# Attention with the two heads of a pair side by side: scores in 64-row tiles, one exponential for both, value matmuls adjacent in column halves

## Chip, cores and metric

The kernel runs on one NeuronCore of a Trainium2 chip. The metric is device time in microseconds (us) of one execution; the median of three runs of the kernel before is 2613.1 us (2609.99 to 2618.43). The profile shows one execution. Engines: PE is TensorE's matmul, PEld its weight load, DVE is VectorE, ACT is ScalarE, POOL is GpSimd, SP is SyncE, which here only issues DMAs.

## The reference, cut to what matters

The program is one layer with two branches: a recurrence (RWKV-7) and an attention with latent projections (MLA), mixed by gates. Sequence 2048, model width 1024. Only the attention is touched. It has 8 heads; each head's query and key have 64 plain features and 32 rotary ones, and the rotary part of the key is the same for all heads; a value has 64 features.

```python
def attend(args):
    qn, qp, b = args
    s = jnp.einsum('bqhd,bkhd->bhqk', qn, k_nope) + jnp.einsum('bqhr,bkr->bhqk', qp, k_pe)
    s = s.astype(jnp.float32) * scale
    q_idx = b * Q_BLOCK + jnp.arange(Q_BLOCK)
    s = jnp.where(key_idx[None, :] <= q_idx[:, None], s, jnp.finfo(jnp.float32).min)
    p = jax.nn.softmax(s, axis=-1).astype(dt)
    return jnp.einsum('bqhk,...' )  # weighted values, per head
```

## The kernel before

Phase 1 (0 to 1160 us) normalises the tokens, projects them and runs the recurrence. Phase 2 is the attention, phase 3 (from 1925 us) the gates and output projections. Everything in float32; where a matmul runs in the faster fp32r form, an operand is split into a leading part (names ending in H or h) and a trailing one (L or l), and a product is the sum of three (hi*hi, lo*hi, hi*lo).

The attention works on 4 pairs of heads, and for each pair on NS = 4 groups g of 512 queries. `queries(i)` (L933 to L980) prepares group i: projections `pq` (mm3, L277 to L279), the leading and trailing parts QH[h], QL[h] of each head (64 plain rows at the top, 32 rotary rows below, one row more for minus the row maximum), then the row maxima: for each head, each 128 queries j and each 512 keys c up to the diagonal a product `pm` of the leading parts (L966), on the diagonal with the causal mask added by a matmul (L969), and a maximum over the keys on DVE (L970). The maxima go through m, mh and `pn` (L978) into row 96 of QH (L979). `keys` (L905 to L917) makes a pair's keys. `attend(i)` (L1018 to L1084) goes through the keys in blocks kb of 128, 4g + 4 of them, and on the diagonal with only the queries that see them. For each head it computes scores transposed, keys on partitions, in three products into `pst` (L1040 to L1042; row 96 subtracts the row maximum), the mask (L1044), the exponential on ACT (L1050); one block later the value matmul into `po` (L1055), in float32, head 0 in the upper and head 1 in the lower column half of the array, and the running sum `acc` of the weights (L1060), on DVE for kb % 5 in (1, 3) and on POOL else. At the end of a group come the sums (L1068, psum_s) and `Ou`; at the end of a pair reciprocals and scaling (L1073 to L1083).

PSUM has 8 banks of 512 float32 per partition: here one for psum_s, one for po, two for pst and four for the tag "mx", which pm, pq, pk, pn and bc2 share. The loop (L1086 to L1106) writes the queries of up to two groups ahead before a group's attend. The order on each engine is set by a scheduler that goes by modelled times and by the pools' buffers; engines take their instructions in that order, and PE never passes one that waits.

## Time and profile before

| | |
|---|---|
| median of 3 runs | 2613.1 us |
| profiled execution: span | 2609.1 us |
| median of the runs less that span | 4.0 us, taken as what lies around the span; so the profiled execution's own time is 2613.1 us |
| busy: PE / DVE / ACT / POOL | 93% / 56% / 36% / 46% |
| attention: from, to, length | 1160, 1925, 765 us |

The busy shares are over the whole span. The granted clock (PEclk) is 1.00 at 2.4 GHz and 0.50 at 1.2 GHz. In the timeline a row is one instruction, or several in a row of the same group (x2); a matmul in float32 leaves two records. Matmuls overlap their ends, so the distance between two starts tells what one costs.

### The profile page before, as it was taken

The numbers are of one execution on the slowest core, as the hardware profiler recorded it, in microseconds if no ns is written. First come the engines' busy times: TensorE is split into PE (matmuls) and PEld (weight loads), VectorE is DVE, ScalarE is ACT, GpSimd is POOL, SyncE is SP. The second block draws the span as 40 slices with busy tenths as digits, with TensorE's granted clock in tenths as the row PEclk, the third lists the DMA queues.
The fourth block names the chain that finished last, engine by engine and source line by source line (L and its number), as shares of the span: only waits on it lengthen the run. The fifth ranks groups of instructions, "written<-read, shape, count | busy, mean of one in ns | idle before, by whom it ended". The sixth has DMA issues, their size and how long they took to land.

```text
span 2609.1 us, 36894 instructions
## 1 busy us (share of the span) xinstructions
PE 2430.6 (93%) x13097; PEld 1714.8 (66%) x13097; DVE 1453.1 (56%) x2527; ACT 945.0 (36%) x1806; POOL 1194.2 (46%) x1426
## 2 busy tenths in 40 slices
PE   7979999899979899998999999989989998999997
PEld 5757677677757667775445545545458886788886
DVE  7166785967677666636555555636343255632443
ACT  4344343433333333242243343323333332333331
POOL 6475665656564646435343343334223323333552
PEclk9989999899989999997999999999999999999999
DMA  6565464535444555443011011021044366543652
GB/s 214 155 208 138 128 202 118 140 84 152 111 125 104 146 135 149 113 130 95 19 38 35 23 37 53 19 99 49 0 140 130 94 210 193 176 135 97 200 179 77
DMA packets 395057, 303.42 MB, mean 116 GB/s; under 512 B 109372, under 2 KB 340856, under 8 KB 388984
## 3 DMA queue, kind: packets, MB, share of 16 engines
q1 hardware_dynamic: 364600, 252.30, 34.0%
q0 software_dynamic: 12992, 44.57, 5.3%
q10 hardware_dynamic: 17280, 4.20, 1.0%
q8 instruction: 103, 1.69, 0.3%
q14 instruction: 82, 0.67, 0.1%
HBM read 227.58 MB, written 73.40 MB: 115 GB/s over the span
## 4 chain that ended last, share of the span: by engine, by line
PE 66%; DVE 16%; DMA 9%; POOL 4%; issue 3%; ACT 2%; SPq 1%; ACTq 0%; POOLq 0%; DVEq 0%
PE po L1055 10%; PE pj L279 7%; PE pj L277 7%; PE pj L278 7%; PE pst L1040 4%; PE pm L966 3%; DVE tq L662 3%; DVE Xg L664 3%; DMA wraw<-in_w_in_dram 3%; PE pz L609 3%; PE pst L1042 3%; PE pst L1041 3%; PE pout L277 2%; PE py L277 2%; PE py L278 2%
## 5 line engine op out<-in xcount | busy, mean ns | idle before, releaser
L277 PE MATMUL pj<-xh,wh 128*128 128x512 f32 (+2 forms) x1344 | 539.3, 401 | 26.3 <-ACT wh L255 9.6
L279 PE MATMUL pj<-xh,wl 128*128 128x512 f32 (+2 forms) x1344 | 541.6, 403 | 3.6 <-POOL wl L256 3.5
L278 PE MATMUL pj<-xl,wh 128*128 128x512 f32 (+2 forms) x1344 | 536.4, 399 | 0.0
L256 POOL TENSOR_TENSOR wl<-wraw,wh 128x512 fp32r<-128x512 f32 (+1 forms) x266 | 345.4, 1300 | 353.3 <-ACT wh L255 325.9
L255 ACT CAST wh<-wraw 128x512 fp32r<-128x512 f32 x392 | 240.7, 614 | 530.3 <-PE pj L278 177.9
L277 PEld LDWEIGHTS pj<-xh,wh 128*128 128x128 f32 (+1 forms) x1344 | 259.5, 193 | 91.7 <-ACT wh L255 16.1
L1060 POOL TENSOR_TENSOR acc<-acc,pt 128x512 f32<-128x512 f32 (+3 forms) x160 | 175.6, 1100 | 292.4 <-ACT pt L1050 276.3
L279 PEld LDWEIGHTS pj<-xh,wl 128*128 128x128 f32 (+1 forms) x1344 | 259.4, 193 | 68.5 <-POOL wl L256 9.0
L278 PEld LDWEIGHTS pj<-xl,wh 128*128 128x128 f32 (+1 forms) x1344 | 259.4, 193 | 55.7 <-issue 1.6
L1050 ACT ACTIVATE pt<-pst 128x512 f32<-128x512 f32 (+3 forms) x288 | 150.9, 525 | 341.9 <-PE pst L1042 189.5
L970 DVE TENSOR_REDUCE mx<-pm 128x1 f32<-128x512 f32 (+2 forms) x320 | 180.3, 605 | 149.6 <-PE pm L966 99.9
L1055 PE MATMUL po<-pt,Vt 128*64 128x512 f32 (+3 forms) x576 | 260.8, 548 | 0.0
L256 DVE TENSOR_TENSOR wl<-wraw,wh 128x512 fp32r<-128x512 f32 x126 | 106.5, 848 | 100.3 <-ACT wh L255 99.9
L1060 DVE TENSOR_TENSOR acc<-acc,pt 128x512 f32<-128x512 f32 (+3 forms) x128 | 91.7, 722 | 112.7 <-ACT pt L1050 103.4
L1040 PEld LDWEIGHTS pst<-QH,KH 97*128 97x128 f32 x312 | 59.0, 189 | 135.4 <-ACT pt L1050 112.1
L1040 PE MATMUL pst<-QH,KH 97*128 97x512 f32 (+2 forms) x312 | 133.4, 428 | 12.4 <-ACT pt L1050 12.4
L1163 DVE SCALAR_TENSOR_TENSOR tg<-tg,py 128x512 f32<-128x512 f32 x64 | 43.8, 685 | 160.9 <-PE py L279 116.2
L662 DVE TENSOR_TENSOR tq<-Xg,Qg 128x30 f32<-128x30 f32 (+7 forms) x240 | 103.4, 431 | 32.6 <-DMA Xg<-d_q 26.6
L1042 PE MATMUL pst<-QH,KL 96*128 96x512 f32 (+2 forms) x312 | 115.1, 369 | 0.0
L1041 PE MATMUL pst<-QL,KH 96*128 96x512 f32 (+2 forms) x312 | 114.8, 368 | 0.0
L277 PE MATMUL py<-BH,wh 128*128 128x512 f32 x256 | 102.9, 402 | 8.2 <-DVE tg L1163 7.8
L966 PE MATMUL pm<-KH,QH 96*128 96x512 f32 (+2 forms) x312 | 108.8, 421 | 0.0
(356 smaller groups left out, 4479.4 us busy)
## 6 DMA issues: line engine op xcount, KB each, us to landing
wraw<-in_w_in_dram SPq DMA_DIRECT2D x320, 256.0 KB
cqt<-d_cq POOLq DMA_DIRECT2D x16, 1024.0 KB, 5.2
wfr<-in_w_o_dram SPq DMA_DIRECT2D x64, 256.0 KB
d_zg<-thg SPq DMA_DIRECT2D x42, 256.0 KB
xl<-d_x POOLq DMA_DIRECT2D x8, 1024.0 KB, 9.4
xh<-d_x POOLq DMA_DIRECT2D x8, 1024.0 KB, 9.5
ring<-in_x_dram SPq DMA_DIRECT2D x32, 256.0 KB
wraw<-in_w_out_a_dram SPq DMA_DIRECT2D x32, 256.0 KB
```

Source lines behind the costliest of these rows:

```text
L255: (ehi.copy if ehi is A else ehi.tensor_copy)(hi, src)
L256: elo.tensor_tensor(lo, src, f32(hi), op=ALU.subtract)
L277: PE.matmul(ps, lhsT=lh, rhs=rh, start=(i == 0), stop=False)
L278: PE.matmul(ps, lhsT=lh, rhs=rl, start=False, stop=False)
L279: PE.matmul(ps, lhsT=ll, rhs=rh, start=False, stop=(stop and i == n - 1))
L662: V.tensor_tensor(t3, Xg[:, 0:m, s_:s_ + 1].to_broadcast([P, m, n]), Qg[:, s_:s_ + 1, s_ + 1:32].to_broadcast([P, m, n]), op=ALU.mult)
L966: PE.matmul(pm[:, 0:w], lhsT=q_h[0:96, j * P:(j + 1) * P], rhs=kh[0:96, c * 512:c * 512 + w], start=True, stop=c < g)
L1040: PE.matmul(ps[:, q0:512], lhsT=kh[0:97, ks_], rhs=q_h[0:97, q0:512], start=True, stop=False)
L1041: PE.matmul(ps[:, q0:512], lhsT=kh[0:96, ks_], rhs=q_l[0:96, q0:512], start=False, stop=False)
L1042: PE.matmul(ps[:, q0:512], lhsT=kl[0:96, ks_], rhs=q_h[0:96, q0:512], start=False, stop=not diag)
L1055: PE.matmul(po[h * HD:(h + 1) * HD, q0:512], lhsT=Vt[p // 3][:, kb, (2 * p % 6 + h) * HD:(2 * p % 6 + h + 1) * HD], rhs=pts[h][:, q0:512], ...
L1060: e.tensor_tensor(acc[h][:, q0:512], acc[h][:, q0:512], pts[h][:, q0:512], op=ALU.add)
```

## The change

The tiles of a pair now hold both heads: head 0 in partitions 0 to 63, head 1 in 64 to 127. QH, QL, KH, KL hold the plain features; the rotary parts go to tiles of their own: QR (leading and trailing part of each head, 32 rows each) against KR4 (the leading rotary key four times), QM (leading part, and the row with minus the maximum) against KR5 (trailing rotary key, and ones). A score tile is then five products per head of 64 or 33 rows, and the two heads' products stand one behind the other in the two row halves of the array. pst, pt, acc, pm, pk, pq, pn and bc2 are tiles of two banks' width, [128, 2, 512]: pst 2 of them, the tag "mx" one (bufs=1). One exponential, one maximum, one running sum handle both heads (DVE for odd kb, POOL for even); values follow two blocks later, two blocks at a time, so that four value matmuls stand together. The mask is added by two products of 64 rows per head. QR and QM are filled by six DMAs per group on SP from a tile `qhl`. The rotary tables, the weights' columns and the place where the mask constants are made change with that.

```diff
-                        pm = psp.tile([P, 512], F32, name="pm", tag=ptag, bufs=pbufs)
-                        PE.matmul(pm[:, 0:w], lhsT=q_h[0:96, j * P:(j + 1) * P], rhs=kh[0:96, c * 512:c * 512 + w],
-                                  start=True, stop=c < g)
-                        if c == g:
-                            PE.matmul(pm[:, w - P:w], lhsT=nmaskT, rhs=identr, start=False, stop=True)
-                        V.tensor_reduce(mx[:, j, c:c + 1], pm[:, 0:w], axis=AX.X, op=ALU.max)
+                    pm = psp.tile([P, 2, 512], F32, name="pm", tag=ptag, bufs=pbufs)
+                    for k, (qt, kt) in enumerate(((QH, kh), (QR, KR4))):
+                        for h in range(2):
+                            PE.matmul(pm[:, h, 0:w], lhsT=qt[HR[h], js], rhs=kt[HR[h], ks_], start=(k == 0),
+                                      stop=(k == 1 and c < g))
+                    if c == g:
+                        for a in range(2):
+                            for h in range(2):
+                                PE.matmul(pm[:, h, w - P:w], lhsT=nmask2[HR[h], a, :], rhs=ident2[HR[h], a, :],
+                                          start=False, stop=(a == 1))
+                    V.tensor_reduce(mx[:, :, j, c], pm[:, :, 0:w], axis=AX.X, op=ALU.max)
...
+            hl = sb.tile([HD, 2, 512], F32R, name="qhl", tag="qhl", bufs=1)
+            split(hl[:, 0], hl[:, 1], ra, A, G)
+            for h in range(2):
+                r = slice(32 * h, 32 * h + 32)
+                nc.sync.dma_start(f32(QR[HD * h:HD * h + 32, :]), f32(hl[r, 0]))
+                nc.sync.dma_start(f32(QR[HD * h + 32:HD * h + HD, :]), f32(hl[r, 1]))
+                nc.sync.dma_start(f32(QM[HD * h:HD * h + 32, :]), f32(hl[r, 0]))
...
-                    PE.matmul(ps[:, q0:512], lhsT=kh[0:97, ks_], rhs=q_h[0:97, q0:512], start=True, stop=False)
-                    PE.matmul(ps[:, q0:512], lhsT=kh[0:96, ks_], rhs=q_l[0:96, q0:512], start=False, stop=False)
-                    PE.matmul(ps[:, q0:512], lhsT=kl[0:96, ks_], rhs=q_h[0:96, q0:512], start=False, stop=not diag)
...
+                for k, (kt, qt, n) in enumerate(((kh, QH, HD), (kh, QL, HD), (kl, QH, HD), (KR4, QR, HD),
+                                                 (KR5, QM, 33))):
+                    for h in range(2):
+                        r = slice(h * HD, h * HD + n)
+                        PE.matmul(pst[:, h, q0:512], lhsT=kt[r, ks_], rhs=qt[r, q0:512], start=(k == 0),
+                                  stop=(k == 4 and not diag))
...
+                A.activation(pt[:, :, q0:512], pst[:, :, q0:512], AF.Exp, scale=scale)
...
-                            e = V if kb % 5 in (1, 3) else G
-                            e.tensor_tensor(acc[h][:, q0:512], acc[h][:, q0:512], pts[h][:, q0:512], op=ALU.add)
+                    if kb:
+                        e = V if kb % 2 else G
+                        e.tensor_tensor(acc[:, :, q0:512], acc[:, :, q0:512], pt[:, :, q0:512], op=ALU.add)
...
-                if len(late) > 1:
+                if len(late) > 2:
+                    late.pop(0)()
                     late.pop(0)()
...
-                for _ in queries(nq, Q[nq % NQ], sb, pp, "mx", 4):
+                for _ in queries(nq, Q[nq % NQ], sb, pp, "mx", 1):
```

The order on PE in the second pair, while the maxima of its fourth group are computed. Before: the maxima (`pm`, each with its own buffer number) of head 0, between the products of the third group's scores (`pst`) and values (`po`).

```order
L966 MATMUL pm_14103<-KH2_12775,QH10_12378 128x512
L966 MATMUL pm_14106<-KH2_12775,QH10_12378 128x256
L969 MATMUL pm_14106<-identr_106,nmaskT_99 128x128
L1040 MATMUL pst_14566<-QH00_12374,KH2_12775 128x512
L1041 MATMUL pst_14566<-QL00_12376,KH2_12775 128x512
L1042 MATMUL pst_14566<-QH00_12374,KL2_12776 128x512
L1055 MATMUL po_14491<-pt_14554,Vt0_10130 64x512
L966 MATMUL pm_14110<-KH2_12775,QH10_12378 128x512
L966 MATMUL pm_14113<-KH2_12775,QH10_12378 128x512
L1040 MATMUL pst_14572<-QH01_12375,KH3_12780 128x512
L1041 MATMUL pst_14572<-QL01_12377,KH3_12780 128x512
L1042 MATMUL pst_14572<-QH01_12375,KL3_12781 128x512
```

One or two maxima stand between any two score tiles. The same place in the changed kernel, at the end of that group's maxima; QM1 holds the row that `pn` makes:

```order
L990 MATMUL pm_14193<-KH1_12796,QH1_12392 128x512 x2
L990 MATMUL pm_14193<-KR4_12249,QR1_12394 128x512 x2
L990 MATMUL pm_14199<-KH1_12796,QH1_12392 128x512 x2
L990 MATMUL pm_14199<-KR4_12249,QR1_12394 128x512 x2
L990 MATMUL pm_14205<-KH1_12796,QH1_12392 128x512 x2
L990 MATMUL pm_14205<-KR4_12249,QR1_12394 128x512 x2
L990 MATMUL pm_14211<-KH1_12796,QH1_12392 128x512 x2
L990 MATMUL pm_14211<-KR4_12249,QR1_12394 128x512 x2
L995 MATMUL pm_14211<-ident2_10122,nmask2_10121 128x128 x4
L1006 MATMUL pn_14225<-identr_10153,mh_14223 1x128 x8
L1069 MATMUL pst_14839<-QM1_12395,KR5_12250 128x512
L1069 MATMUL pst_14852<-QM1_12395,KR5_12250 128x512
```

Here the last of ten maxima steps stand one behind the other, and after them the transposed maxima and the product that uses them; each pm tile is the same two banks.

The order on DVE at the same place. Before, the end of head 1's maxima:

```order
L970 TENSOR_REDUCE mx_14146<-pm_14173 128x1
L970 TENSOR_REDUCE mx_14146<-pm_14176 128x1
L1060 TENSOR_TENSOR acc_14496<-acc_14496,pt_14673 128x128
L970 TENSOR_REDUCE mx_14146<-pm_14179 128x1
L970 TENSOR_REDUCE mx_14146<-pm_14182 128x1
L970 TENSOR_REDUCE mx_14146<-pm_14186 128x1
L1060 TENSOR_TENSOR acc_14502<-acc_14502,pt_14680 128x128
L970 TENSOR_REDUCE mx_14146<-pm_14189 128x1
L970 TENSOR_REDUCE mx_14146<-pm_14192 128x1
L970 TENSOR_REDUCE mx_14146<-pm_14195 128x1
L973 TENSOR_REDUCE m1_14199<-mx_14146 128x4
```

Running sums (`acc`) stand between. In the changed kernel:

```order
L997 TENSOR_REDUCE mx_14108<-pm_14165 128x2
L997 TENSOR_REDUCE mx_14108<-pm_14171 128x2
L997 TENSOR_REDUCE mx_14108<-pm_14177 128x2
L997 TENSOR_REDUCE mx_14108<-pm_14183 128x2
L997 TENSOR_REDUCE mx_14108<-pm_14193 128x2
L997 TENSOR_REDUCE mx_14108<-pm_14199 128x2
L997 TENSOR_REDUCE mx_14108<-pm_14205 128x2
L997 TENSOR_REDUCE mx_14108<-pm_14211 128x2
L1000 TENSOR_REDUCE m1_14221<-mx_14108 128x8
L1002 TENSOR_SCALAR mh_14223<-m1_14221 128x8
```

Ten maxima of both heads follow each other without another operation; the wait of each for its pm tile and of the next pm tile for it makes one chain.

The order on PE in the steady middle, scores and values of two heads. Before, of two heads one behind the other:

```order
L1040 MATMUL pst_14582<-QH00_12374,KH2_12775 128x512
L1041 MATMUL pst_14582<-QL00_12376,KH2_12775 128x512
L1042 MATMUL pst_14582<-QH00_12374,KL2_12776 128x512
L1055 MATMUL po_14491<-pt_14570,Vt0_10130 64x512
L966 MATMUL pm_14123<-KH2_12775,QH10_12378 128x512
L966 MATMUL pm_14126<-KH2_12775,QH10_12378 128x512
L1040 MATMUL pst_14588<-QH01_12375,KH3_12780 128x512
L1041 MATMUL pst_14588<-QL01_12377,KH3_12780 128x512
L1042 MATMUL pst_14588<-QH01_12375,KL3_12781 128x512
L1055 MATMUL po_14491<-pt_14576,Vt0_10130 64x512
```

In the changed kernel, one key block of both heads and the values of two:

```order
L1069 MATMUL pst_13327<-QH2_12396,KH0_12259 128x512 x2
L1069 MATMUL pst_13327<-QL2_12397,KH0_12259 128x512 x2
L1069 MATMUL pst_13327<-QH2_12396,KL0_12260 128x512 x2
L1069 MATMUL pst_13327<-QR2_12398,KR4_12249 128x512 x2
L1069 MATMUL pst_13327<-QM2_12399,KR5_12250 128x512 x2
L1086 MATMUL po_13237<-pt_13306,Vt0_10155 64x512 x2
L990 MATMUL pm_12838<-KH0_12259,QH0_12388 128x512 x2
L990 MATMUL pm_12838<-KR4_12249,QR0_12390 128x512 x2
L1086 MATMUL po_13237<-pt_13325,Vt0_10155 64x512 x2
```

Five pairs of products take the place of six single ones, and the four value matmuls of two blocks stand near each other, here with a maximum's products among them.

## Rows read from the trace of the kernel before

**Rows 1.** Page: the chain that ended last, share of the span by line.

```profile
PE po L1055 10%; PE pj L279 7%; PE pj L277 7%; PE pj L278 7%; PE pst L1040 4%; PE pm L966 3%; DVE tq L662 3%; DVE Xg L664 3%; DMA wraw<-in_w_in_dram 3%; PE pz L609 3%; PE pst L1042 3%; PE pst L1041 3%; PE pout L277 2%; PE py L277 2%; PE py L278 2%
```

**Rows 2.** Windows: from:to length, busy us PE PEld DVE ACT POOL, PEclk, DMA, GB/s.

```profile
1160.00:1192.00 32.00, 23.03 (x205) 17.76 (x204) 24.62 (x42) 12.24 (x25) 16.97 (x34) 0.81 0.45 124
1192.00:1200.00 8.00, 8.00 (x22) 5.26 (x20) 0.85 (x2) 3.64 (x8) 2.75 (x7) 0.50 0.53 133
1214.00:1224.00 10.00, 8.60 (x27) 6.23 (x27) 7.57 (x17) 1.17 (x2) 0.00 (x0) 0.51 0.05 7
1224.00:1750.00 526.00, 522.31 (x1927) 264.25 (x1925) 292.59 (x493) 190.09 (x349) 210.65 (x186) 1.00 0.11 35
1160.00:1925.00 765.00, 733.29 (x2790) 378.56 (x2789) 414.35 (x689) 265.36 (x493) 295.46 (x286) 0.97 0.15 46
```

**Rows 3.** Timeline, PE, steady middle: start us, us, engine line op out<-in xcount.

```profile
1508.34 0.51 PE L1040 MATMUL pst<-QH,KH 97*128 97x512 f32 x1
1508.69 0.40 PE L1041 MATMUL pst<-QL,KH 96*128 96x512 f32 x1
1508.92 0.40 PE L1042 MATMUL pst<-QH,KL 96*128 96x512 f32 x1
1509.25 1.07 PE L1055 MATMUL po<-pt,Vt 128*64 128x512 f32 x2
1510.25 0.49 PE L1040 MATMUL pst<-QH,KH 97*128 97x512 f32 x1
```

**Rows 4.** Timeline, PE: one long wait late in the stage, narrow blocks at its end.

```profile
1762.42 0.58 PE L1040 MATMUL pst<-QH,KH 97*128 97x256 f32 x1 [10.43 <-ACT pt L1050]
...
1911.61 0.33 PE L1040 MATMUL pst<-QH,KH 97*128 97x128 f32 x1
...
1912.20 0.65 PE L1055 MATMUL po<-pt,Vt 128*64 128x256 f32 x2
1912.78 0.33 PE L1040 MATMUL pst<-QH,KH 97*128 97x128 f32 x1
```

**Rows 5.** Timeline, PE: products in halves of the array, in phase 1 and attention.

```profile
205.97 1.71 PE L609 MATMUL pz<-AR,BK 64*128 64x128 f32 x16
...
313.53 1.16 PE L609 MATMUL pz<-AR,BK 64*128 64x128 f32 x8
...
1208.41 0.82 PE L1055 MATMUL po<-pt,Vt 128*64 128x256 f32 x5
1208.92 0.64 PE L1068 MATMUL psum_s<-acc,osel 128*64 128x512 f32 x1
```

**Rows 6.** Groups in attention by line and shape: xcount, busy us, mean ns, idle before.

```profile
L970 DVE TENSOR_REDUCE mx<-pm 128x1 f32<-128x512 f32 x224 | 148.6, 686 | 111.7 <-PE pm L966 99.9 <-PE pm L969 11.3
L1060 POOL TENSOR_TENSOR acc<-acc,pt 128x512 f32<-128x512 f32 x104 | 134.5, 1296 | 162.4 <-ACT pt L1050 146.4 <-DVE m L973 5.8 <-DVE acc L1060 5.4
...
L954 POOL TENSOR_TENSOR qra<-qra,qrb 32x512 f32<-32x512 f32 x32 | 46.3, 1447 | 20.9 <-DVE qrb L953 19.9
...
L979 ACT CAST QH<-pn 1x512 fp32r<-1x512 f32 x30 | 17.2, 573 | 34.7 <-PE pn L978 34.5
```

**Rows 7.** Lines L228 and L236, 1024 wide: count, ns min/median/max, first and last start.

```profile
L228 ACT ACTIVATE xjunk<-xt x12: 1040/1057/1058, 21.3 to 517.1; 128x1024 bf16<-128x1024 f32 x12
...
L236 DVE SCALAR_TENSOR_TENSOR xt<-xt,xrs,g_rep x12: 1268/1285/1737, 25.4 to 521.7; 128x1024 f32<-128x1024 f32 x12
```

**Rows 8.** Timeline, hand-overs between PE and DVE among the first group's maxima.

```profile
1181.60 0.31 PE L969 MATMUL pm<-identr,nmaskT 128*128 128x128 f32 x1
...
1181.95 0.42 DVE L970 TENSOR_REDUCE mx<-pm 128x1 f32<-128x256 f32 x1 [0.52 <-PE pm L969]
...
1182.43 0.80 PE L966 MATMUL pm<-KH,QHx 96*128 96x512 f32 x1
```

**Rows 9.** Waits in attention: who <- for whom, us, times, longest us.

```profile
PEld pm L966 <- DVE mx L970: 44.9, 68, 0.8
```

**Rows 10.** DMA issues in attention: out<-in queue xcount, KB each, us to landing.

```profile
KH<-d_kr POOLq DMA_DIRECT2D x4, 256.0 KB, 4.8
```

More of the change, by code (lines that the diff above doesn't have):

```diff
@@ L895, in hybrid_layer @@
         KH, KL = [], []
+        KR4 = kp.tile([P, T], F32R, name="KR4")
+        KR5 = kp.tile([P, T], F32R, name="KR5")
+        for r in range(4):
+            G.dma_start(KR4[32 * r:32 * r + 32, :], d_kr[:, 0, :])
+        for h in range(2):
+            G.dma_start(KR5[HD * h:HD * h + 32, :], d_kr[:, 1, :])
+            V.memset(f32(KR5[HD * h + 32:HD * h + 33, :]), 1.0)
         def key_tiles(pool, i):
@@ new lines, in queries @@
+            kh = KH[p % 2]
+            pq = psp.tile([P, 2, 512], F32, name="pq", tag=ptag, bufs=pbufs)
+            for k in range(2):
+                ps = pq[:, k, :]
+                mm3(ps, [(qws[p][k][c], (cqt[:, c, 0, :], cqt[:, c, 1, :])) for c in range(2)])
+                if k == 0:
+                    split(QH, QL, ps, A, V)
+                    yield
+            ra = sb.tile([HD, 512], F32, name="qra", tag="qra", bufs=1)
+            rb = sb.tile([HD, 512], F32, name="qrb", tag="qrb", bufs=1)
@@ L972, in queries @@
-                m1 = sb.tile([P, 4], F32, name="m1", tag="m1", bufs=2)
-                V.tensor_reduce(m1, mx[:, :, 0:g + 1], axis=AX.X, op=ALU.max)
-                mh = sb.tile([P, 4], F32R, name="mh", tag="mh", bufs=2)
-                V.tensor_scalar(mh, m1, -1.0, None, op0=ALU.mult)
-                pn = psp.tile([P, 512], F32, name="pn", tag=ptag, bufs=pbufs)
-                for j in range(4):
-                    PE.matmul(pn[0:1, j * P:(j + 1) * P], lhsT=mh[:, j:j + 1], rhs=identr, start=True, stop=True)
@@ L979, in queries @@
-                A.copy(q_h[96:97, :], pn[0:1, :])
-                yield
-        for i in range(2):
-            key_tiles(kp, i)
+                    PE.matmul(pn[0:1, h, j * P:(j + 1) * P], lhsT=mh[:, h, j:j + 1], rhs=identr, start=True, stop=True)
+            for h in range(2):
+                A.copy(QM[HD * h + 32:HD * h + 33, :], pn[0:1, h, :])
+            yield
+        key_tiles(kp, 0)
         qst = ExitStack()
@@ L1002, in hybrid_layer @@
         bsel = sb.tile([P, NS, P], F32R, name="bsel")
-        bself = sb.tile([P, NS, P], F32, name="bself", tag="pt", bufs=6)
+        bself = sb.tile([P, NS, P], F32, name="bself", tag="pt", bufs=4)
         G.memset(bself, 0.0)
@@ L1020, in attend @@
             p, g = divmod(i, NS)
[L1021 to L1022 removed]
+            QH, QL, QR, QM = Q[i % NQ] if i else Q0
+            kh, kl = KH[p % 2], KL[p % 2]
             if g == 0:
@@ new lines, in attend @@
+                if diag:
+                    for a in range(2):
+                        for h in range(2):
+                            PE.matmul(pst[:, h, q0:q0 + P], lhsT=ident2[HR[h], a, :], rhs=nmask2[HR[h], a, :],
+                                      start=False, stop=(a == 1))
+                if kb == 0:
+                    pt = sb.tile([P, 2, 512], F32, name="acc", tag="acc", bufs=2)
+                    acc = pt
+                else:
+                    pt = sb.tile([P, 2, 512], F32, name="pt", tag="pt", bufs=4)
@@ L1104, in hybrid_layer @@
                 kp = st.enter_context(tc.tile_pool(name="p2k", bufs=1, reuse_waits="tile"))
-                for k in range(2, 4):
-                    key_tiles(kp, k)
+                key_tiles(kp, 1)
     with ExitStack() as st:
```

154 lines of the change are left out of this document (71 added, 83 removed).

## The prediction

> **What bounds the kernel now.** I read the page first: the chain that ended last, by line, is almost all TensorE (PE) matmuls, and the attention's value matmuls lead it with 10% [rows 1]. Then I read busy time by stage. Attention is the stretch from 1160 to 1925 us, 765 us: 32 us in which the first group's maxima are taken with little beside them, some 722 us for four pairs of heads, and 10 us of end. In the long middle PE is busy 522.3 of 526.0 us at the full granted clock, 1.00, while VectorE (DVE) is busy 56%, ScalarE (ACT) 36% and GpSimd (POOL) 40% [rows 2]. So between 1224 and 1750 us PE alone is the bound. One pair takes (765 - 32 - 10) / 4 = 181 us.
>
> What a pair's 181 us are made of stands in the timeline. A head's three score products start 0.35 and 0.23 us apart, the values' matmul follows 0.33 later and holds PE for 1.00 us; from one head's scores to the next head's are 1.91 us [rows 3], so a full key block of two heads costs 3.8 us; the narrowest, 128 queries with the values of the 256-wide block before it, takes 1.17 us a head [rows 4]. A pair has 40 key blocks: 28 of 512 queries and 4 each of 384, 256 and 128. The row maxima (L966 to L970) are small and spread between: PE waits for a maximum 68 times in the whole stage, 44.9 us in all, never longer than 0.8 us [rows 9].
>
> **What the change saves on PE.** Scores: 6 products of 97 or 96 rows per block become 5 pairs of products of at most 64 rows. If two row halves run side by side a pair costs what one product costs, 0.23 us [rows 3]: 28 x 5 x 0.23 = 32 us, and about 8 for the narrow blocks. Side by side is what the nearest rows show: sixteen 64-row products of alternating halves (L609) took 1.71 us, 0.11 each, with other pairs under way, and eight of one half took 1.16, 0.14 each [rows 5]; that alone does not prove a factor of two, since 128 columns are short. For column halves the evidence is better: at 1208.41 five value records, two heads of one block, take 0.51 us until the next matmul starts, where one head's 256-wide values alone take 0.58 [rows 4, 5]. So values: 28 x 0.96 = 27 us and 7 for narrow blocks. Masks on the 16 diagonal blocks, two pairs each at 0.11: 3.5. First product and switch from scores to values, 0.12 and 0.09 more than a plain step [rows 3], 40 times: 8. Row sums 4, projections of queries and keys 60 matmuls at 0.23: 14, small ones 3. Fifteen maxima steps that lie among them (below), 0.5 each: 8. Sum 115. The same kind of sum for before (56 x 1.91 = 107, 24 narrow ones at about 1.4 between 1.17 and 1.65: 34, and 45 for the rest) gives 186 where 178 are measured (181 less a quarter of the stage's one long wait, 10.4 us before 1762.42 [rows 4]); scaled so, 115 becomes 110 us a pair. If nothing else were in the way the pair would fall from 181 to about 125 with its other maxima.
>
> **What it adds: the chain through one buffer.** The maxima tiles were four of one bank; they are now one tile of two banks (bufs=1), which `pk`, `pq`, `pn` and `bc2` share. A new step can start on PE only when DVE has read the last. In the order, 15 of a pair's 40 steps stand between key blocks and are covered by them; 25 stand with nothing between (6 for the second group, 10 and 9 for the others), each run ended by `pn` and by the score product with QM that waits for it. In before 1 to 3 maxima stand between any two heads' score products and there are four buffers. PE works in order, so in a run nothing else of it can go on.
>
> Price of one such step, for 512 keys. DVE: a 512-wide maximum of one head takes 0.686 us [rows 6], so two heads at most 1.37; a 1024-wide DVE operation takes 1.285 [rows 7]. No 1024-wide maximum stands in the trace; I take 1.25, a little under the nearest row, since a maximum writes almost nothing. Hand-overs: from a matmul's end (1181.60 + 0.31) to the maximum's start 0.04, and 0.06 from the maximum's end to the next matmul [rows 8]. PE: two pairs of products until the last result is out, 0.23 + 0.40 at full clock [rows 3]; at half clock one 512-wide product takes 0.80 [rows 8], the two 1.23. So a step costs 1.98 at full clock and 2.58 at half. With the narrow steps and masks, 25 steps and the last maximum of each of three runs: about 50 us a pair at full clock, 66 at half.
>
> Which clock? In a run PE is busy 0.6 to 0.8 of every 2 us. The rows like it: 1160 to 1192, where the first group's maxima go through two buffers, PE busy 23 of 32 us, mean clock 0.81, and after it 8 us of dense PE work still at 0.50; 1214 to 1224, maxima in a row after a wait, clock 0.51 with PE busy 8.6 of 10 [rows 2]. Both say that the level of 1.2 GHz (0.50) comes in such stretches and stays for some microseconds of dense work. I take runs that begin at full and go on at half clock: 61 us. Dense work at half clock after a run: 5 us of work take 2.5 more; two or three runs: 6 us.
>
> The Trainium skill has a rule on this, in "TensorE: Matmul & The Clock Gate", section "A second HAM failure mode: psum-queue depth-cycling": a PE that idles briefly between groups of matmuls as it goes round PSUM banks makes the clock swing between its two levels, and throughput falls. By that rule the runs sit at half clock; the two stretches of [rows 2] agree, though neither has a single buffer. Its rule against the change as a whole is in "TensorEngine Tiling (Array Packing)", section "PSUM Bottleneck": tiling quickens TensorE but not what empties PSUM, which may become the bound. By it the 25 steps, not the products, decide; the trace of before shows DVE at 56% and cannot show it yet.
>
> Two more waits. After each run two DVE steps, `pn`, and two ACT copies of 0.57 each [rows 6] with hand-overs, 2.6 us, stand before the product with QM: 3 a pair, 8 us. And the rotary parts of the queries now pass through six DMAs on SP: two 512-wide DVE multiplications of about the maximum's 0.69, a POOL sum of 1.45, an ACT cast of about 0.6, another POOL operation of the same kind [rows 6], then a landing. The nearest landing is 4.8 us for 256 KB [rows 10]; these are 64 KB each, so between 1.5 and 4.8, and I take 3: 8 us until the first maximum can start, of which the order gives 5 to 9 us of key blocks. What is queued behind that first maximum on PE is the next key block and its values. Cost 0 to 4 a group; I take 6 a pair.
>
> Costed at nothing: the exponential of both heads in one, 1.06 us for 1024 [rows 7], lies under 2.3 us of PE per block. The running sum of a block, 2.4 on POOL (at most twice 1.296) or 1.24 on DVE in turn [rows 6, 7], 3.7 for two blocks under 4.6 of PE; with that cover gone it would be the next bound. Fewer reductions, copies and casts on engines that wait anyway are worth nothing.
>
> **Sum.** A pair: 110 + 61 + 6 + 8 + 6 = 191 us against 181. Four pairs 764, less 10 since the last has no next queries, 37 for the start (32, and 5 for one buffer instead of two), 10 for the end: 801 against 765, +36. On the profiled span of 2609.1 us that is 2645; the median of the runs is 4.0 us above the span, so 2649, say 2650 us. The pair's break-even is 182: runs, waits and lost clock may cost 72 us, and I have 81.
>
> **Rivals.** *The runs stay at full clock.* Then 110 + 50 + 4 + 8 = 172 a pair, 688 + 37 = 725, 40 us less: 2573. For it: in 1224 to 1750 the clock was at 1.00 throughout, maxima and all, and the stretches at 0.5 each followed a wait of PE of over 1 us. Against: those stretches had more PE work in them than the runs will have. It decides if the granted clock in the runs stays above 0.9; the step then costs under 2.0 us. This ends on the faster side.
>
> *The maxima slide under the scores.* If the steps of the runs were covered like the other 15, a pair costs PE's own 125 to 130, and the time is about 2400. Against: the order has nothing to put between, and PE takes its instructions in order.
>
> *Halves do not run side by side.* Then scores cost 28 x 5 x 0.23 + 8 = 40 us more and values 33, 4 x 73 = +290: about 2930. Against it the column halves of [rows 5]; for it only that no 512-wide pair of row halves stands in the trace. It decides if the second head's product starts 0.2 us after the first.
>
> **How the numbers follow.** Forecast case 0.61, its own range 2600 to 2715 (step at half clock 2.3 to 2.8, DMA wait 0 to 4 a group, the 110 good to 6); rival one 0.27, 2540 to 2605; rival two 0.05; rival three 0.07. A measurement of this kernel tells 0.3%, 8 us, from no change. Same: 0.04 of the forecast case and 0.04 of the first rival. Slower: 0.55 of the forecast case and 0.07. Faster: 0.02 of the forecast case, 0.23 of rival one and 0.05, in all 0.30. The range 2550 to 2715 leaves out the second and third rival and a little of both ends.
>
> **What would show it.** Right: per pair two or three stretches of 12 to 25 us with PE under half busy, DVE near 60% with maxima alone, the granted clock near 0.5, PE's largest waits on DVE mx and on ACT QM; between them key blocks of 2.3 us. A key block of 3 us or more says that halves do not overlap; runs at 1.00 say the first rival; no such stretches, the second. Wrong above all if the saving on PE is larger than 71 us a pair or if a single step costs much under 2 us.

## The result and the profile after

The changed kernel takes 2745.8 us (median of 4 runs, 2728.4 to 2756.0) against 2611.6 us of before in the same comparison: a ratio of 1.052, 95% interval 1.048 to 1.057. It is slower by 5.2%; forecast were 2650 us and slower, with a range that ended at 2715. The direction and the mechanism were right, the size was not.

The profiled execution took 2756.0 us, its span is 2754.0. From its page, busy time, and the rows of PE and of the granted clock in 40 slices, in tenths:

```profile
PE 2407.4 (87%) x14313; PEld 1738.2 (63%) x14313; DVE 1382.8 (50%) x2205; ACT 886.4 (32%) x1591; POOL 1111.6 (40%) x1304
...
PE   7979989899798989957796797787779998999998
...
PEclk9989899899999999977796787777779999999999
```

PE has fallen from 93% to 87% of a longer span. Slices 18 to 30 are the attention: the granted clock, before almost all 9 there, stands at 6, 7 or 8 in all of them but one.

The windows of the changed kernel: first the stage from the first score product to the last row sum, then five neighbouring stretches, maxima in a row and key blocks by turns (columns as in [rows 2]).

```profile
1225.20:2058.30 833.10, 663.69 (x3767) 369.32 (x3766) 314.47 (x331) 193.55 (x253) 189.38 (x116) 0.78 0.11 35
1498.80:1526.20 27.40, 13.70 (x70) 7.79 (x68) 12.24 (x13) 0.57 (x1) 0.00 (x0) 0.56 0.00 0
1526.20:1566.70 40.50, 37.53 (x228) 21.39 (x230) 14.96 (x15) 14.07 (x18) 15.48 (x10) 0.90 0.19 50
1566.70:1591.90 25.20, 12.05 (x62) 6.59 (x58) 11.81 (x12) 0.57 (x1) 0.00 (x0) 0.61 0.00 0
1591.90:1660.20 68.30, 65.64 (x400) 36.08 (x400) 27.70 (x28) 24.89 (x32) 23.51 (x14) 0.95 0.16 51
1660.20:1677.00 16.80, 8.40 (x52) 5.40 (x52) 7.32 (x9) 0.57 (x1) 0.00 (x0) 0.62 0.00 0
```

The stage is 833 us long; before it was 723 (1192.1 to 1915.5, PE busy 706, clock 0.98). PE is busy 664 of 833 us at a mean clock of 0.78. The three stretches with ACT and POOL all but empty are the runs of maxima that the order shows: 27.4, 25.2 and 16.8 us, PE half busy, clock 0.56 to 0.62, only DVE at work beside it. The two stretches between have 0.90 and 0.95.

A run in the timeline of PE:

```profile
1502.53 0.50 PE L990 MATMUL pm<-KH,QH 64*128 64x512 f32 x2 [0.52 <-DVE mx L997]
1502.87 0.39 PE L990 MATMUL pm<-KR,QR 64*128 64x512 f32 x2
1504.58 0.79 PE L990 MATMUL pm<-KH,QH 64*128 64x512 f32 x2 [1.32 <-DVE mx L997]
...
1509.03 0.79 PE L990 MATMUL pm<-KH,QH 64*128 64x512 f32 x2 [0.79 <-DVE mx L997]
...
1511.58 0.80 PE L990 MATMUL pm<-KH,QH 64*128 64x512 f32 x2 [1.32 <-DVE mx L997]
```

A step of 512 keys takes 2.05 us at full clock (1502.53 to 1504.58) and 2.55 at half (1509.03 to 1511.58); 1.98 and 2.58 were forecast. The wait at its end is the maximum of 1024 values and two hand-overs. VectorE's and the other wide operations by line and shape, which answer to [rows 6] and [rows 7]:

```profile
L997 DVE TENSOR_REDUCE mx<-pm 128x2 f32<-128x1024 f32 x112 | 137.2, 1225 | 172.8 <-PE pm L990 141.3 <-PE pm L995 23.7 <-PE pst L1069 7.7
L1091 POOL TENSOR_TENSOR acc<-acc,pt 128x1024 f32<-128x1024 f32 x48 | 113.8, 2372 | 368.7 <-DVE acc L1091 328.3 <-ACT pt L1081 31.1 <-DVE mx L997 9.3
...
L1081 ACT ACTIVATE pt<-pst 128x1024 f32<-128x1024 f32 x96 | 98.0, 1025 | 127.3 <-PE pst L1069 112.6 <-PE pst L1074 14.4
```

The maximum takes 1.225 us (1.25 forecast). The longest waits of the stage:

```profile
ACT QM L1008 <- PE pn L1006: 308.4, 15, 30.0
PEld pm L990 <- DVE mx L997: 168.5, 104, 2.0
...
PE pm L990 <- DVE mx L997: 115.8, 100, 1.3
```

ACT waits for `pn` up to 30 us, while PE stands in a run. PE's own wait for `mx` has grown from 68 times and 0.8 us at most [rows 9] to over 100 times and up to 2.0 us.

That the halves of the array do run side by side, a steady stretch of PE's timeline shows:

```profile
1624.17 0.51 PE L1069 MATMUL pst<-QH,KH 64*128 64x512 f32 x2
1624.52 0.40 PE L1069 MATMUL pst<-QL,KH 64*128 64x512 f32 x2
...
1625.45 0.40 PE L1069 MATMUL pst<-QH,KH 64*128 64x512 f32 x2
...
1626.71 1.08 PE L1086 MATMUL po<-pt,Vt 128*64 128x512 f32 x4
...
1629.22 0.50 PE L1069 MATMUL pst<-QH,KH 64*128 64x512 f32 x2
```

Each x2 is the products of both heads; a block's five pairs take 1.28 us (1624.17 to 1625.45), 0.23 from pair to pair, as one product did in [rows 3]. Two key blocks with their values take 5.05 us to 1629.22, of which 0.49 are a maximum's products: 2.3 a block against 3.8. The third rival is out.

### The profile page after: what moved, and what is told of

It is laid out like the page before. It is cut to its first block, busy times and chain, and to the rows that moved or that the text cites. A ratio compares the mean times of both kernels' runs of the same rounds, so it can differ in the third digit from the quotient of the medians.

```text
span 2754.0 us, 38637 instructions
## 1 busy us (share of the span) xinstructions
PE 2407.4 (87%) x14313; PEld 1738.2 (63%) x14313; DVE 1382.8 (50%) x2205; ACT 886.4 (32%) x1591; POOL 1111.6 (40%) x1304
## 3 DMA queue, kind: packets, MB, share of 16 engines
q8 instruction: 113, 1.85, 0.3%
## 5 line engine op out<-in xcount | busy, mean ns | idle before, releaser
L1091 POOL TENSOR_TENSOR acc<-acc,pt 128x1024 f32<-128x1024 f32 (+1 forms) x64 | 134.2, 2097 | 388.7 <-DVE acc L1091 336.4
L997 DVE TENSOR_REDUCE mx<-pm 128x2 f32<-128x1024 f32 (+3 forms) x160 | 170.5, 1065 | 234.7 <-PE pm L990 141.3
L990 PE MATMUL pm<-KH,QH 64*128 64x512 f32 (+3 forms) x312 | 94.4, 585 | 117.3 <-DVE mx L997 115.8
L1081 ACT ACTIVATE pt<-pst 128x1024 f32<-128x1024 f32 (+2 forms) x144 | 126.3, 881 | 193.8 <-PE pst L1069 112.6
L1091 DVE TENSOR_TENSOR acc<-acc,pt 128x1024 f32<-128x1024 f32 (+1 forms) x80 | 83.1, 1039 | 166.3 <-ACT pt L1081 87.8
L990 PEld LDWEIGHTS pm<-KH,QH 64*128 64x128 f32 x312 | 39.7, 234 | 183.0 <-DVE mx L997 168.5
L1086 PE MATMUL po<-pt,Vt 128*64 128x512 f32 (+3 forms) x576 | 142.4, 567 | 2.0 <-ACT pt L1081 2.0
L1008 ACT CAST QM<-pn 1x512 fp32r<-1x512 f32 x30 | 17.2, 573 | 308.8 <-PE pn L1006 308.4
L656 DVE TENSOR_TENSOR Xg<-Xg,tq 128x30 f32<-128x30 f32 (+7 forms) x240 | 103.7, 432 | 6.6
L270 PE MATMUL py<-BL,wh 128*128 128x512 f32 x256 | 102.8, 402 | 0.0
```

The costliest lines, as they stand in the source:

```text
L270: PE.matmul(ps, lhsT=lh, rhs=rl, start=False, stop=False)
L656: V.tensor_tensor(Xg[:, 0:m, s_ + 1:32], Xg[:, 0:m, s_ + 1:32], t3, op=ALU.add)
L990: PE.matmul(pm[:, h, 0:w], lhsT=qt[HR[h], js], rhs=kt[HR[h], ks_], start=(k == 0), stop=(k == 1 and c < g))
L997: V.tensor_reduce(mx[:, :, j, c], pm[:, :, 0:w], axis=AX.X, op=ALU.max)
L1081: A.activation(pt[:, :, q0:512], pst[:, :, q0:512], AF.Exp, scale=scale)
L1086: PE.matmul(po[h * HD:(h + 1) * HD, q0:512], lhsT=Vt[p // 3][:, kb, (2 * p % 6 + h) * HD:(2 * p % 6 + h + 1) * HD], rhs=pt[:, h, q0:512], ...
```

## What the experiments showed

Theory A: the maxima's one buffer makes a serial chain of products and maximum; PE idles in it, its clock falls, and the key blocks after it pay too. Rival B: the loss is in the 64-row products and in the rotary parts' way through DMAs. The table gives the median, the ratio to before with its interval, and by the windows view the stage from first score product to last row sum, PE's idle time in it and its clock.

| kernel | us | ratio, 95% | stage us | PE idle us | PEclk |
|---|---|---|---|---|---|
| before | 2611.6 | 1 | 723 | 18 | 0.98 |
| changed | 2745.8 | 1.052 [1.048, 1.057] | 833 | 169 | 0.78 |
| 1: before, one maxima buffer | 2943.7 | 1.130 [1.127, 1.133] | 1065 | 207 | 0.78 |
| 2: changed, two single banks | 2643.2 | 1.014 [1.011, 1.018] | 734 | 46 | 0.82 |
| 3: changed, copies for DMAs | 2727.2 | 1.047 [1.044, 1.050] | 822 | 168 | 0.78 |
| 4: changed, products repeated | 2824.3 | 1.084 [1.081, 1.087] | 904 | 159 | 0.78 |
| 5: changed, two double banks | 2528.9 | 0.971 [0.969, 0.974] | 615 | 55 | 0.93 |
| 6: changed, four single banks | 2523.4 | 0.969 [0.966, 0.972] | 622 | 49 | 0.93 |
| 7: before, values adjacent alone | 2492.3 | 0.956 [0.953, 0.959] | 602 | 43 | 0.96 |
| 8: before, two maxima buffers | 2710.3 | 1.041 [1.036, 1.046] | 819 | 58 | 0.93 |
| 9: as 1, PE filled | 2921.0 | 1.122 [1.118, 1.126] | 1036 | 57 | 0.97 |
| 10: as 6, with DMAs | 2510.7 | 0.964 [0.962, 0.967] | 598 | 42 | 0.97 |
| 11: as 5, with DMAs | 2502.9 | 0.962 [0.959, 0.965] | 597 | 48 | 0.96 |
| 12: as 11, first group by copies | 2508.0 | 0.964 [0.962, 0.966] | 598 | 46 | 0.96 |

**1. The old kernel with one buffer.**

```diff
-                for _ in queries(nq, Q[nq % NQ], sb, pp, "mx", 4):
+                for _ in queries(nq, Q[nq % NQ], sb, pp, "mx", 1):
...
-                    bc = pp.tile([P, 512], F32, name="bc2", tag="mx", bufs=4)
+                    bc = pp.tile([P, 512], F32, name="bc2", tag="mx", bufs=1)
```

> The kernel before with one single-bank buffer instead of four for the maxima's tag (pm, pq, pk, pn, bc2); three banks stay empty, nothing else changes. Theory A (one buffer makes a serial chain of products and maxima in which PE idles, and the clock falls): in the order 215 of 320 head-steps now follow another with nothing between; each waits about 0.8 us (0.69 maximum and 0.1 hand-over): 170 us more, some of it given back where before waited too (45), some lost to the clock: 2740 to 2860 us, granted clock in attention well under 0.97. Theory B (the loss comes from the 64-row products and the rotary DMAs, and the buffers hardly matter): within 30 us of 2612.

2944 us: more than theory A said, 340 above before. The edit changes the number of buffers alone, so they do not "hardly matter", as rival B had it; that the 64-row products are not the loss is shown by 5, 6, 10 and 11, which keep them. The order changed with the buffers: up to 14 maxima, of one head each, now stand in a row on PE, where in before it is at most four, and eight once (more than the one or two of the excerpt). No run has the old order with one buffer, so for this kernel the two are not told apart. A run of 18 records of maxima products, in the windows view and then two steps of it in PE's timeline:

```profile
1630.70:1652.40 21.70, 11.04 (x19) 4.91 (x19) 9.22 (x16) 0.00 (x0) 0.00 (x0) 0.50 0.00 0
```

Two steps:

```profile
1647.07 0.80 PE L966 MATMUL pm<-KH,QH 96*128 96x512 f32 x1 [0.78 <-DVE mx L970]
1648.65 0.79 PE L966 MATMUL pm<-KH,QH 96*128 96x512 f32 x1 [0.78 <-DVE mx L970]
```

The level of 0.50 holds throughout, and a step of one head takes 1.58 us. The forecast of 0.8 us a wait was right; it had too little for the clock: over the stage PE is busy 292 us at half clock, between the runs as well as in them.

**8. The old kernel with two buffers** (the same two lines with 2).

> The kernel before with two single-bank buffers for the maxima's tag instead of four (two banks stay empty). Between four (2603) and one (2944): theory A says that with two the product of the next step runs under the maximum of the last, but a run of up to 14 head-steps is bound by VectorE at about 0.74 us each against 0.25 of PE: 2640 to 2760 us, clock between 0.90 and 0.97. Theory B: within 30 of 2605.

2710: in the range. Four, two and one buffers give 2603 to 2612, 2710 and 2944.

**2. The changed kernel with two single-bank tiles.**

```diff
-                    pm = psp.tile([P, 2, 512], F32, name="pm", tag=ptag, bufs=pbufs)
+                    for h in range(2):
+                        pm = psp.tile([P, 512], F32, name="pm", tag=ptag, bufs=pbufs)
...
+                        V.tensor_reduce(mx[:, h, j, c:c + 1], pm[:, 0:w], axis=AX.X, op=ALU.max)
-                    V.tensor_reduce(mx[:, :, j, c], pm[:, :, 0:w], axis=AX.X, op=ALU.max)
```

> The changed kernel with the maxima's tag as two tiles of one bank, one head each (pk, pq, pn, bc2 too), in place of one tile of two banks; the same banks in all. The maxima's two products of a head then stand one behind the other, not in pairs. Theory A: one head's products run under the other's maximum, so a step of both heads costs about 1.5 us at full and 1.85 at half clock instead of 2.05 and 2.55: the runs fall from 269 to about 190 us and the clock is lost less often: 2600 to 2670 us. Theory B: 2730 to 2760.

2643, 103 us below the changed kernel with the same banks, although the maxima's products lose their pairing; PE's idle time falls from 169 to 46 us. The runs are nearly as long as before (up to 9 steps of both heads in a row, 11 in the changed kernel), so here it is the second buffer and not another order that takes the idle time away. A step at half clock now takes 2.00 us (1517.14 to 1519.14; 1.85 forecast), and the stage's clock stays low, at 0.82:

```profile
1517.14 0.79 PE L987 MATMUL pm<-KH,QH 64*128 64x512 f32 x1 [0.18 <-DVE mx L993]
...
1519.14 0.79 PE L987 MATMUL pm<-KH,QH 64*128 64x512 f32 x1 [0.18 <-DVE mx L993]
```

**3. Copies for the rotary DMAs.**

```diff
-                nc.sync.dma_start(f32(QR[HD * h:HD * h + 32, :]), f32(hl[r, 0]))
-                nc.sync.dma_start(f32(QR[HD * h + 32:HD * h + HD, :]), f32(hl[r, 1]))
-                nc.sync.dma_start(f32(QM[HD * h:HD * h + 32, :]), f32(hl[r, 0]))
+                A.copy(QR[HD * h:HD * h + 32, :], f32(hl[r, 0]))
+                G.tensor_copy(QR[HD * h + 32:HD * h + HD, :], f32(hl[r, 1]))
+                A.copy(QM[HD * h:HD * h + 32, :], f32(hl[r, 0]))
```

> The changed kernel with the six DMAs that fill QR and QM per group replaced by four copies on ACT and two on POOL. Theory A: PE's waits for these DMAs (some 17 us in all, 2.0 to 2.6 us each) go, and with them the half clock that follows each, at most 30 us: 2700 to 2740 us. Theory B (the rotary parts' way through DMAs is the main loss): under 2670.

2727: 19 us less, in A's range, and B's "under 2670" is out. But the gain did not come in A's way. The waits for the DMAs (17.4 us) are gone, yet the stage's idle time (168 us, 169 in the changed kernel) and its clock (0.78) are the same: PE now waits 12.4 us, in eight waits, for an exponential. The longest, of 3.1 us, come where that exponential stands on ACT behind the group's four copies, and half clock follows them too:

```profile
1466.23 1.12 PE L1086 MATMUL po<-pt,Vt 128*64 128x256 f32 x4 [3.10 <-ACT pt L1081]
```

So this run shows that DMAs or copies matter little here; it does not show what the waits for the DMAs cost.

**4. More products in the chain, to hold the clock.**

```diff
+                    for _ in range(2):
+                        for h in range(2):
+                            PE.matmul(pm[:, h, 0:w], lhsT=QH[HR[h], js], rhs=kh[HR[h], ks_], start=True, stop=True)
                     for k, (qt, kt) in enumerate(((QH, kh), (QR, KR4))):
```

> The changed kernel with each maxima step's first pair of products made three times into the same tile (the first two are overwritten): 160 x 2 pairs of matmuls more for PE, 75 us at full clock, all in the chain. Theory A with the clock as a large part (176 us of dense work at half clock, 88 us lost there, and steps of 2.55 instead of 2.05 us): if the extra products hold the clock at 1.00, a step costs 2.05 + 0.47 = 2.52 us, as much as now at half clock, and the dense parts get up to 80 us back: 2660 to 2720. If they do not hold it, a step costs 2.55 + 0.86 = 3.4: 2830 to 2850. If the clock plays no part (rival): 75 us more, 2820.

2824, 79 us more, the rival's number. But the run's clock did not hold, so the question was not put. The windows view over one run, and then two of its steps in PE's timeline:

```profile
1506.50:1535.00 28.50, 17.91 (x94) 11.37 (x92) 9.65 (x10) 0.00 (x0) 0.00 (x0) 0.57 0.00 1
```

Two steps:

```profile
1519.43 1.22 PE L990 MATMUL pm<-KH,QH 64*128 64x512 f32 x4 [0.79 <-DVE mx L1000]
...
1522.83 1.22 PE L990 MATMUL pm<-KH,QH 64*128 64x512 f32 x4 [1.32 <-DVE mx L1000]
```

PE is busy 17.9 of 28.5 us and the clock is 0.57; a step takes 3.4 us. The total is 6 us under the range for this case; the reason was not followed up.

**9. PE kept busy beside the maximum.** Kernel 1 has three empty banks, so a matmul that nobody reads can run while VectorE reads the one buffer.

```diff
+                last = None
...
                         V.tensor_reduce(mx[:, j, c:c + 1], pm[:, 0:w], axis=AX.X, op=ALU.max)
+                        if dmy and last is not None:
+                            PE.matmul(dmy[0][0:1, 0:384], lhsT=last, rhs=Vt[1][:, 0:3, :].rearrange("p a b -> p (a b)"),
+                                      start=True, stop=True)
+                        last = mx[:, j, c:c + 1]
...
+        dmy.append(pp.tile([P, 512], F32, name="dmy", tag="dmy", bufs=1))
```

> The kernel with the old scores and one single-bank buffer for the maxima (2944 us), with one matmul more behind each maxima step: one column by 384 float32 values into an empty bank, nobody reads it, and it can start when the step before has its maximum; so PE has about 0.7 us of work while DVE takes each maximum. It adds work and removes no wait. Theory A with the clock as its own part (that kernel's attention has 461 us at half clock, half of it lost, 230 us): PE stays busy in the runs, the clock stays at 1.00, and although the matmuls cost some 60 to 100 us where nothing is waited for, the time falls to 2740 to 2860 us. Rival (the idle time alone costs, the clock plays no part): 60 to 200 us more, 3000 to 3140.

2921: 23 us less than kernel 1, with 282 matmuls and 226 us of PE time more. The range was missed above, but the rival's 3000 to 3140 is out. A run of it in the windows view, and then one step in PE's timeline:

```profile
1475.60:1486.00 10.40, 9.05 (x31) 2.84 (x31) 4.37 (x9) 0.57 (x1) 0.77 (x1) 1.00 0.01 2
```

One step, the added matmul on line 975:

```profile
1476.69 0.50 PE L969 MATMUL pm<-KH,QH 96*128 96x512 f32 x1
1477.12 0.81 PE L975 MATMUL dmy<-Vt,mx 128*1 128x384 f32 x2
1477.98 0.39 PE L969 MATMUL pm<-KH,QH 96*128 96x256 f32 x1
```

PE is busy 9.1 of 10.4 us at 1.00, and a step takes 1.29 us instead of 1.58 (1476.69 to 1477.98). The stage has a clock of 0.97 instead of 0.78 and 57 us of idle time instead of 207; what that gives back, the added matmuls (0.80 us each in a step, more than the wait they fill, and without use between key blocks) take again. The maxima stand in nearly the same rows as in kernel 1, and added work alone could only have cost time; so the clock has a price of its own; its amount is not measured cleanly by this. The forecast had that price too high: it took half of all 461 us at half clock as lost, but PE was busy in only 292 of them, so no more than 146 us could come back, not 230.

**5 and 6. The banks dealt out anew.** One score tile instead of two, two double-bank maxima tiles (5) or four single ones (6), values one block late, copies for DMAs.

```diff
-                pst = pp.tile([P, 2, 512], F32, name="pst", tag="st", bufs=2)
+                pst = pp.tile([P, 2, 512], F32, name="pst", tag="st", bufs=1)
...
-                if len(late) > 2:
-                    late.pop(0)()
+                if len(late) > 1:
                     late.pop(0)()
...
-                for _ in queries(nq, Q[nq % NQ], sb, pp, "mx", 1):
+                for _ in queries(nq, Q[nq % NQ], sb, pp, "mx", 2):
```

> The changed kernel with the banks dealt out anew: two tiles of two banks for the maxima's tag and one for the scores (was one and two); values one block late instead of two at a time; QR and QM by copies. In the order no more than five maxima steps stand in a row, where up to eleven did. Theory A (the one-buffer chain of maxima and the clock it costs are the whole loss): the maxima go under key blocks; a pair costs about 125 us of PE, and 40 waits of 0.1 to 0.5 us for the exponential of a score tile, now alone in its buffer: 130 to 145 us, clock near 1.00: 2420 to 2520 us. Rival C (whichever tile has one buffer makes the chain: now scores and exponential, 160 times 1.1 us with little beside): 2650 or more.

> As the run with two tiles of two banks, but the maxima's tag as four tiles of one bank, one head each, the maxima's products of a head one behind the other. Theory A: 40 x 0.46 us more PE a pair than paired products, at most 18 us a pair, and deeper buffering: 2440 to 2560 us. Rival C: 2650 or more.

2529 and 2523: both faster than before, 217 to 222 us below the changed kernel, with all its 64-row products, so rivals B and C are out. In 5 the time is a little over the range, in 6 in it. Buffers, order and the moment of the values change together here: mostly two maxima steps stand in a row, at most five in 5, where the changed kernel has up to 11. Of PE's 49 idle us in 6, 43 are waits for an exponential. ACT's timeline shows a group's copies ahead of one:

```profile
1503.99 0.63 ACT L247 CAST qhl<-qra 64x512 fp32r<-64x512 f32 x1 [0.36 <-POOL qra L968]
1504.65 0.62 ACT L973 CAST QR<-qhl 32x512 fp32r<-32x512 f32 x1
...
1506.33 0.61 ACT L975 CAST QM<-qhl 32x512 fp32r<-32x512 f32 x1
1506.96 1.02 ACT L1076 ACTIVATE pt<-pst 128x1024 f32<-128x1024 f32 x1
```

**10 and 11. DMAs again, with the new banks** (the lines of 3 the other way round).

> The kernel with 64-row scores, one score tile, four single-bank maxima tiles (2523 us), with QR and QM filled by the six DMAs again instead of copies. In the run with copies the exponential of a score tile waited up to 2.5 us behind four copies of 0.6 us on ACT, once per group, and PE with it. If that is what the row halves lose against the kernel with six full products (2492): 16 x 1.5 to 2.4 us less, 2480 to 2500 us, and below 2492 with the clock that comes back. If the first maximum of a group waits for the DMAs instead (as in the changed kernel, 2 to 2.6 us): 2515 to 2535.

> The same with two maxima tiles of two banks (2529 us with copies). As the run with four tiles of one bank: 2485 to 2510 if the copies on ACT were the loss, 2515 to 2540 if the DMAs' landing is waited for in their place.

2511 and 2503: 13 and 26 us less than with copies. 11 fell in the range, 10 between its two cases. In 11 the maxima stand under key blocks, at full clock, as PE's timeline shows:

```profile
1508.00 0.33 PE L990 MATMUL pm<-KH,QH 64*128 64x128 f32 x2
1508.24 0.51 PE L1069 MATMUL pst<-QH,KH 64*128 64x512 f32 x2
...
1509.61 1.08 PE L1086 MATMUL po<-pt,Vt 128*64 128x512 f32 x4
```

**7. One part of the change alone.** Old scores, old maxima and four single banks; one exponential, one sum and adjacent values for both heads; one score tile.

```diff
+                pst = pp.tile([P, 2, 512], F32, name="pst", tag="st", bufs=1)
...
+                A.activation(pt[:, :, q0:512], pst[:, :, q0:512], AF.Exp, scale=scale)
...
                     for h in range(2):
                         PE.matmul(po[h * HD:(h + 1) * HD, q0:512],
                                   lhsT=Vt[p // 3][:, kb, (2 * p % 6 + h) * HD:(2 * p % 6 + h + 1) * HD],
-                                  rhs=pts[h][:, q0:512], start=(kb == 0), stop=(kb == nk - 1))
+                                  rhs=pt[:, h, q0:512], start=(kb == 0), stop=(kb == nk - 1))
```

> The kernel before with one part of the change alone: one exponential and one running sum for both heads and the two heads' value matmuls adjacent; scores stay six products of 97 and 96 rows, maxima keep four single banks, the score tile of two banks has one buffer. Theory A: values fall from about 68 to 34 us a pair, 136 us in all, less waits for the one score tile (160 times 0.1 to 0.5): 2480 to 2570 us. If the halves gained nothing (rival), 2620 or more. The difference to the kernels with 64-row scores is what the row halves are worth: 16 us a pair by PE's busy time, about 60.

2492.3, ratio 0.956: the fastest kernel of the study. By PE's timeline the value matmuls fall from 272 to 146 us in the stage. Against it the row halves of 11 give 24 us of score products (214 instead of 238) and only 5 us of stage, 597 against 602, less than the 60 expected: the maxima's products take 98 us instead of 90, and PE's idle time is 48 instead of 43. They lose more than that in the start (12).

**12. The start.**

```diff
+            if i == 0:
+                for h in range(2):
+                    r = slice(32 * h, 32 * h + 32)
+                    A.copy(QR[HD * h:HD * h + 32, :], f32(hl[r, 0]))
+                    G.tensor_copy(QR[HD * h + 32:HD * h + HD, :], f32(hl[r, 1]))
+                    V.tensor_copy(QM[HD * h:HD * h + 32, :], f32(hl[r, 0]))
+            else:
```

> The kernel with 64-row scores, one score tile and two maxima tiles of two banks (2503 us), where the very first group's QR and QM are filled by copies on ACT, POOL and DVE, all others by DMAs. In the changed kernel PE waits 9.6 and 2.6 us for these DMAs at the start, queued on SP behind others. If that is what the start has lost (PE's first score product at 1220 us in that kernel, 1207 to 1212 with copies, 1203 with the old scores): 8 to 14 us less, 2489 to 2495, level with the best so far (2492). If another wait takes its place: 2500 to 2505.

2508, with an interval that overlaps with that of 11: no gain. The expectation rested on a misreading: the times of the first score product that it compares hold the end of phase 1 too, which differs between executions whatever the kernel (the last `pz` product of phase 1 starts between 1051.5 and 1071.0 us). From that product to the first score product it is 155.3 us in the changed kernel, 154.7 in 11, 154.0 in 12, and with copies for all groups 156.7 (3), 155.1 (5) and 153.2 (6); with the old scores it is 135.2 (before) and 135.6 (7). So the 64-row kernels lose some 20 us in the start, and by copies they do not get them back. PE's timeline before the first score product, in the changed kernel and then in this one:

```profile
1209.45 0.44 PE L990 MATMUL pm<-KR,QRx 64*128 64x128 f32 x1 [9.57 <-DMA QRx<-qhl]
1212.50 0.44 PE L990 MATMUL pm<-KR,QRx 64*128 64x128 f32 x1 [2.61 <-DMA QRx<-qhl]
```

Kernel 12, PE, then ACT and DVE:

```profile
1190.56 0.47 PE L997 MATMUL pm<-KR,QRx 64*128 64x128 f32 x1 [3.43 <-POOL QRx L978]
...
1201.24 0.69 PE L997 MATMUL pm<-KH,QHx 64*128 64x384 f32 x2 [7.01 <-DVE mx L1004]
...
1199.96 0.30 ACT L247 CAST kwh<-kraw 128x128 fp32r<-128x128 f32 x1 [10.47 <-DMA kraw<-in_w_ukv_dram]
...
1200.29 0.29 DVE L248 TENSOR_TENSOR kwl<-kraw,kwh 128x128 fp32r<-128x128 f32 x1 [7.22 <-ACT kwh L247]
```

The wait for the rotary DMAs is gone, and a wait of 7.0 us for a maximum has come in its place. That maximum stands on DVE behind the splitting of key weights (`kwl`), and these weights wait for a DMA of their own. In kernel 3 DVE waits 6.8 us at the same place.

## Why the prediction missed

The sum against the profiled execution, in us over all pairs. The stretches come from the windows view, runs up to the end of `pn`; half clock is twice one less the granted clock, times the length, and costs half of itself where PE is busy; PE's work is what is left of the stage's 833 us.

| term | forecast | measured |
|---|---|---|
| runs with what follows them to the QM product | 276 | 272 (12 runs) |
| PE's work on key blocks, at full clock | 430 | 456 |
| half clock outside the runs | 24 | 72 (143 us at half) |
| waits outside the runs | 24 | 34 |
| 1160 us to the first score product | 37 | 65 |

The differences add up to 108; 2756 less 2650 is 106. (2756.0 is the slowest of the four runs; their median is 96 above the forecast. It also lies 2.0 us above its span, where the forecast added 4.0.)

- **Right: the chain.** Its place, the step's price at both clock levels, and its sum. In the runs 227 of 272 us were at half clock; 61 us a pair came from a mixture near that. The Trainium skill's rule in "TensorEngine Tiling (Array Packing)", section "PSUM Bottleneck", held in the runs, where the maximum that empties the tile takes 1.225 of a step's 2.05 us; it held with the one buffer only: kernel 11 has the same products and maxima and takes 2503 us. Experiments 1, 2, 5 and 8 show the chain.
- **The step that failed: "Dense work at half clock after a run: 5 us of work take 2.5 more; two or three runs: 6 us."** It cost 18 us a pair. There are three runs a pair, which the forecast itself counted elsewhere; three times 2.5 would have been 7.5. After a run the level of 0.50 stayed 4 to 12 us, 7.5 in the mean, not 5: some 90 of the 143 us. The rest came after ten shorter waits, which I had priced by their length alone: eight for the rotary DMAs, of 1.7 to 3.0 us, and two of 1.3 and 1.4 us for an exponential, each followed by 3.4 to 6.9 us at half clock. A wait for the rotary DMAs in PE's timeline, and what follows it:

```profile
1492.68 0.46 PE L990 MATMUL pm<-KR,QR 64*128 64x512 f32 x1 [2.01 <-DMA QR<-qhl]
...
1493.71 0.62 PE L1069 MATMUL pst<-QR,KR 64*128 64x512 f32 x1
...
1495.48 0.63 PE L1069 MATMUL pst<-QL,KH 64*128 64x512 f32 x2
1495.91 0.62 PE L1069 MATMUL pst<-QH,KL 64*128 64x512 f32 x2
```

  The wait is 2.01 us; from 1493.71 to the next run at 1498.80 the products take 0.6 us and more and are 0.43 apart: 5.1 us at half clock, half of it lost. So this wait cost its length and more than as much again. The same rule of the Trainium skill that I cited ("TensorE: Matmul & The Clock Gate", section "A second HAM failure mode: psum-queue depth-cycling") says that the price of the changing clock is paid between the bursts; I took it for the runs and not for what lies between them. The trace agrees, with 72 us lost outside the runs, though this wait was for a DMA and not for a bank.
- **Mis-sized: the start**, 28 us. Some 13 of them are phase 1, whose last `pz` product starts at 1069.9 us in this execution and at 1056.9 in before; kernels 3, 5, 6 and 12 have it at 1051.5 to 1057.3, so this is not the change. The other 15 are the change's: the way from that product to the first score product grew by 20 us, where I had 5 for one buffer instead of two. PE waits 9.6 and 2.6 us of it for the rotary DMAs on SP's queue (the rows of experiment 12), which I had at nothing; but with copies the way is as long, so the DMAs alone are not the cause, and what would shorten it stays open.
- **Mis-sized: PE's work**, 26 us. I scaled 115 us a pair down to 110, by a sum for before that came out 5% high; unscaled it would have been 450 for 456 measured. A small part was not foreseen at all: nine times other products, of a maximum or of the queries' projection, stand between the two heads' values, which then take 0.9 to 1.0 us one behind the other.
- **First rival (full clock): out**, by the clock of the runs; **second (maxima under the scores): out** for this order, but kernels 5, 6, 10 and 11 are that case once the banks are dealt differently, at 2503 to 2529 where it said 2400; **third: out.** The range was drawn from the forecast's own bounds; it had no room for the clock and the start being wrong together.

Not settled: how the loss divides between waiting and clock. The trace puts about 72 us outside the runs and some 45 in them (0.5 us a step) on the clock; the two experiments made for it held the clock not at all (4), or only with other work added (9). Nor is it settled how much lies in the number of buffers and how much in the order that the scheduler makes for them; only kernel 2 keeps the order nearly as it was.

## To carry over

Ask of a change that makes tiles wider how many buffers are left in each PSUM tag, and whether the order still has work to put between two uses of one; here the packed kernel took 2746 us with one maxima tile and 2503 with two and the order that they allow, against 2612 before. In this kernel the single buffer was better with the tile whose reader is covered by other matmuls (scores and exponential), the several with the one that has a chain behind it. Compare the starts of stages from a mark inside the same execution, not from the span's start. A wait of PE of 2 us was not priced by its length alone: look at the granted clock of what follows.
